# Layer with mLSTM and stick-breaking attention: gate rows computed from unit 35 on through small DRAM tensors, and k projected before q in the first half

## The chip, the core and the metric

The kernel runs on one core of one Trainium2 chip. The metric is device time in microseconds (us): the median of 3 runs, 694.9 us before the change (694.86 to 695.47). The names of the engines are those of the profile: PE is TensorE, DVE is VectorE, ACT is ScalarE, POOL is GpSimd; SP only issues DMAs. A trailing q (SPq, POOLq) marks the instruction queue of an engine.

## What is computed

One layer for 512 tokens of width 1024. The input is RMS-normed and projected by one wide matrix; two mixers work on the result, and their outputs are gated, summed, projected and added to the input.

```python
h = rmsnorm(x, norm_w)
(mq, mk, mv, mi, mf, mo, mz, sq, sk, sv, sz, gates) = split(h @ w_in + b_in)
# mLSTM: 4 heads of 256, q and k through a causal conv; 4 + 4 gate columns
log_i, log_f = mi, log_sigmoid(mf)
#   per head h~ = (decay-weighted q k^T) v / max(|den|, exp(-m_t)), m_t the running maximum
# stick-breaking attention: 8 heads of 128, q and k RMS-normed per head
qs, ks = rmsnorm(to_heads(sq), ..), rmsnorm(to_heads(sk), ..)
#   a[t,s] = sigmoid(z_ts) * prod_{s<j<t}(1 - sigmoid(z_tj)),  s < t
x = x + (g_m * (y_m @ w_proj_m) + g_s * (y_s @ w_proj_s)) @ w_out
```

What the change touches: the gate rows of the mLSTM (the running sum b of log_f, the running maximum m, and what is derived from them), and the order in which q and k of the first four attention heads are made.

## The kernel before

**Units.** All projections are cut into units of 24 matmuls of 128x128 by 128x512. Every fp32 operand is split into a high and a low fp32r part, and three products replace one (`mm3`, L90 to L93). A unit's weights, 512 KB, are loaded by SP into a tile `stg` (3 buffers, up to four units ahead); ACT copies the high part `wh` and DVE subtracts to get the low part `wl` (L96, L97), two units ahead of use. The units are, in this order: 0 to 3 q, 4 to 7 k, 8 to 11 v and 12 to 15 z of attention heads 0 to 3; 16 to 31 the same for heads 4 to 7; 32 to 51 o, z, v, q, k of the first mLSTM pair of heads; 52 to 71 the second pair; then the merge gates, the two branch projections and the output projection.

**What sets the order.** The program is written out in a hand-made order; each engine runs its own instructions in that order and waits only on semaphores. The loop at L1236 takes unit c: it evacuates the result of unit c-1, runs what was put off to this unit (`later`, `defer`), emits loads and splits ahead, then the first half of the unit's matmuls, then one step of every generator in `act` (attention heads, mLSTM heads, the gate chain; in the units of REST they pause), then the second half. So PE gets a few small matmuls of a generator between two halves of dense work. `pend` says from which unit a generator may start: `SB_START` for attention heads, `M_START` for mLSTM heads, and GATES_START = 4 for the gate chain `gates`.

**The gate chain before (L574 to L657).** Unit 4: 16 matmuls give the gate pre-activations as rows, 36 partitions by 512 tokens. Then, one step per unit: four PE transposes to 128 tokens by 16 (L592); Abs, Exp and Sigmoid on ACT; 21 small DVE instructions for the log-sigmoid (L603 to L612); four PE transposes back to rows (L616); two DVE scans over 512 tokens (L621, L626); differences, a split copy `rb2` of the row b - m; then eight PE transposes and one small matmul (L646 to L649) bring c = i - b, m and the block ends of b into columns (`c_lag`, `em`, `bs`). It ends in unit 10. Each mLSTM head then spreads its row of `rb2` over 128 partitions by one matmul with a selector `sel` (L751) and a DVE copy (L753); POOL masks it (L758), ACT exponentiates.

**q and k of the attention heads.** `qk_group` adds the bias (L346) into token-major tiles; ACT squares them, POOL makes the reciprocal norms `rq`, `rk`; k is scaled on DVE (L368), q's norm goes into the sigmoid's scale later. To use them a head needs them turned. Most are turned by `turn` (L381): DVE transposes 32x32 blocks into `ty`, 16 DMAs of 32 KB move the blocks to `tz`, and the head splits from there. In the set TURNED k of heads 0 and 1 is missing: those two heads turn k by four PE transposes each (L437).

Of the kernel before, what the change touches and what calls it, by code (L numbers as in the profile page):

```python
# [15 lines left out]
T = 512  # L16
# [10 lines left out]
SB_START = [10, 13, 16, 20, 26, 28, 32, 34]  # L27
M_START = [52, 56, 70, 76]
GATES_PREP, GATES_START = 3, 4
TURNED = {("q", 0, 0), ("q", 0, 1), ("q", 1, 0), ("q", 1, 1), ("k", 0, 1), ("k", 1, 1)}  # L30
# [5 lines left out]
def tile_hybrid_layer(  # L36
# [27 lines left out]
    tiny = pool("tiny", 4)  # L64
    psd = pool("psd", 4, space=bass.MemoryType.PSUM)
# [252 lines left out]
    class SbSet:  # L318
# [18 lines left out]
        def qk_group(self, name, c0):  # L337
# [4 lines left out]
            def evac(tb, ps):  # L342
# [6 lines left out]
                def norm():  # L349
# [8 lines left out]
                    if name == "q":  # L358
# [3 lines left out]
                        if tb == TB - 1:  # L362
                            defer(1, lambda: self.turn(name, 0))
                    else:
                        def scale():
# [3 lines left out]
                            if tb == TB - 1:  # L369
                                done.add(("k", self.s))  # L370
                                defer(1, lambda: self.turn(name, 1))
                        defer(1, scale)

                if tb < 2 or name == "q" and self.s == 0:
                    norm()
                else:
                    defer(1, norm)

            tok_group(w_in, c0 + 512 * self.s, h_sta, evac, name == "q" and self.s == 0, c0 + 512 * self.s, row)

        def turn(self, name, g):  # L381
# [8 lines left out]
            def move():  # L390
# [152 lines left out]
    sel = cst.tile([128, NH, 128], FR, name="sel")  # L543
    rb2 = cst.tile([128, T], FR, name="rb2")
# [6 lines left out]
    def gates_fill():  # L551
        wg = blk("P5", FR, (KT, 128), name="wg")
        nc.gpsimd.memset(wg.bitcast(F32), 0.0)

        sel32 = blk("y", shape=(NH, 128), name="sel32", p=36)
        nc.gpsimd.memset(sel32, 1.0)
        for r in (slice(0, 4), slice(32, 36)):
            nc.gpsimd.affine_select(out=sel32[r], in_=sel32[r], compare_op=OP.is_equal, fill=0.0, base=0,
                                    channel_multiplier=1, pattern=[[-1, 4], [0, 128]])
        nc.gpsimd.memset(sel.bitcast(F32), 0.0)  # L560
        nc.gpsimd.memset(rb2.bitcast(F32), 0.0)
        wg_t.extend([wg, sel32])

    def gates_prep():
        wg, sel32 = wg_t
# [5 lines left out]
        nc.vector.tensor_copy(sel[0:4], sel32[0:4])  # L571
        nc.vector.tensor_copy(sel[32:36], sel32[32:36])

    def gates():  # L574
# [12 lines left out]
        gi = g2[0:4, :]  # L587
        yield

        fp = att_ps()  # L590
# [7 lines left out]
        nc.vector.tensor_copy(f, fp[:, 0:16])  # L598
# [13 lines left out]
        nc.vector.scalar_tensor_tensor(f, f, 0.0, u, op0=OP.min, op1=OP.subtract)  # L612
        yield
        lp = att_ps()
        for j in range(TB):
            nc.tensor.transpose(lp[0:4, j * 128:(j + 1) * 128], f[:, 4 * j:4 * j + 4], ident)  # L616
        f = row("gl")
        nc.vector.tensor_copy(f, lp[0:4, :])
        yield
        m = row("gm")  # L620
        nc.vector.tensor_tensor_scan(m, f, gi, 0.0, op0=OP.add, op1=OP.max)  # L621
        msk = row("gk")
        nc.vector.memset(msk, 1.0)
        nc.vector.memset(msk.rearrange("p (b t) -> p b t", b=TB)[:, :, 0:1], 0.0)
        b = row("gp")
        nc.vector.tensor_tensor_scan(b, msk, f, 0.0, op0=OP.mult, op1=OP.add)  # L626
        yield
        rb = row("gu")
        nc.vector.tensor_tensor(rb, b, m, op=OP.subtract)
        nc.vector.tensor_copy(rb2[0:4], rb)  # L630
        nc.vector.tensor_tensor(rb2[32:36], rb, rb2[0:4].bitcast(F32), op=OP.subtract)
        c = row("gw")
        nc.vector.tensor_tensor(c, gi, b, op=OP.subtract)
# [669 lines left out]
```

## Time and profile before

| | us |
|---|---|
| median of 3 runs | 694.9 |
| profiled execution | 695.12 |
| its span, first to last instruction | 693.4 |
| PE busy | 684.5 |
| DVE busy | 472.9 |
| ACT busy | 334.6 |
| POOL busy | 122.3 |

The span is what the views of the profile cover; the profiled execution's time is 1.7 us longer than it. Matmuls are pipelined: a matmul's shown duration (some 390 ns for 512 columns) overlaps the next one's, so what an instruction takes of PE's time is read from the distance between the starts of neighbours, not from its duration.

### The profile page before, as it was taken

To read this page: it belongs to the slowest core of one execution; us is meant where nothing else is said; L and a number is where in the kernel's file an instruction comes from. 1 tells how busy PE (TensorE), PEld (TensorE's weight loads), DVE (VectorE), ACT (ScalarE), POOL (GpSimd) and SP (SyncE) were. 2 spreads that over 40 slices of the span, in tenths; PEclk is the share of its full clock that TensorE was granted. 3 is DMA by queue.
4 is the path that set the end of the run, shared out by engine and by line. 5 is a ranking of instruction groups with operands and counts; after the bars stand their busy time and mean duration, and the time that the engine had idled before them with its cause. 6 is when DMAs were issued, how large, how long until landed. Compare 5 with 4: busy or idle time off the path is not lost.

```text
span 693.4 us, 9382 instructions
## 1 busy us (share of the span) xinstructions
PE 684.5 (99%) x3172; PEld 569.9 (82%) x3172; DVE 472.9 (68%) x835; ACT 334.6 (48%) x629; POOL 122.3 (18%) x273
## 2 busy tenths in 40 slices
PE   7999999999999999999999999999999999999997
PEld 5888788888888888888888888888888888888876
DVE  6847997867997884479844738995353364445996
ACT  6244355475554643244466434447554343344451
POOL 5422122265440310000011110001112000111021
PEclk9999999999999999999999999999999999999999
DMA  7423534525553534333332343433223456579334
GB/s 248 138 88 104 149 117 124 150 61 159 153 150 99 144 107 133 92 91 92 91 92 61 82 116 99 115 92 104 79 61 87 118 174 199 159 169 217 124 83 130
DMA packets 111288, 84.10 MB, mean 121 GB/s; under 512 B 8302, under 2 KB 95240, under 8 KB 111240
## 3 DMA queue, kind: packets, MB, share of 16 engines
q1 hardware_dynamic: 108312, 76.82, 38.7%
q0 software_dynamic: 2784, 6.56, 4.9%
q8 instruction: 25, 0.41, 0.2%
q14 instruction: 23, 0.19, 0.1%
q10 hardware_dynamic: 144, 0.13, 0.1%
HBM read 65.12 MB, written 2.10 MB: 97 GB/s over the span
## 4 chain that ended last, share of the span: by engine, by line
PE 88%; DVE 1%; DMA 1%; ACT 0%; issue 0%; DVEq 0%; SPq 0%
PE dps L91 26%; PE dps L92 26%; PE dps L93 26%; PE aps L92 3%; PE aps L93 3%; PE aps L91 3%; DMA stg<-in_w_in_dram 1%; PE aps L805 1%; PE aps L807 1%; PE aps L806 1%; PE aps L437 0%; DVE wl L97 0%; DVE gp L626 0%; DVE gm L621 0%; PE aps L751 0%; DVE kraw L368 0%
## 5 line engine op out<-in xcount | busy, mean ns | idle before, releaser
L97 DVE TENSOR_TENSOR wl<-stg,wh 128x1024 fp32r<-128x1024 f32 x92 | 112.4, 1221 | 105.9 <-ACT wh L96 105.5
L91 PE MATMUL dps<-hh,wh 128*128 128x512 f32 x448 | 175.0, 391 | 0.0
L93 PE MATMUL dps<-hh,wl 128*128 128x512 f32 x448 | 174.5, 389 | 0.0
L92 PE MATMUL dps<-hl,wh 128*128 128x512 f32 x448 | 174.4, 389 | 0.0
L96 ACT ACTIVATE wh<-stg 128x1024 fp32r<-128x1024 f32 x92 | 96.8, 1052 | 58.8 <-PE dps L93 35.1
L93 PEld LDWEIGHTS dps<-hh,wl 128*128 128x128 f32 x448 | 84.1, 188 | 17.8
L91 PEld LDWEIGHTS dps<-hh,wh 128*128 128x128 f32 x448 | 84.1, 188 | 16.9
L92 PEld LDWEIGHTS dps<-hl,wh 128*128 128x128 f32 x448 | 84.2, 188 | 16.8
L91 PE MATMUL dps<-wh,hh 128*128 128x512 f32 x224 | 87.9, 393 | 0.0
L93 PE MATMUL dps<-wh,hl 128*128 128x512 f32 x224 | 87.3, 390 | 0.0
L92 PE MATMUL dps<-wl,hh 128*128 128x512 f32 x224 | 87.3, 390 | 0.0
L93 PEld LDWEIGHTS dps<-wh,hl 128*128 128x128 f32 x224 | 42.0, 188 | 9.0
L91 PEld LDWEIGHTS dps<-wh,hh 128*128 128x128 f32 x224 | 42.1, 188 | 8.3
L92 PEld LDWEIGHTS dps<-wl,hh 128*128 128x128 f32 x224 | 42.1, 188 | 8.2
L697 DVE SCALAR_TENSOR_TENSOR acc<-tmp,vec,acc 128x511 f32<-128x511 f32 (+2 forms) x48 | 36.0, 750 | 1.7
L700 ACT ACTIVATE tmp<-acc 128x512 f32<-128x512 f32 x16 | 10.1, 634 | 50.8 <-DVE acc L697 50.8
L462 POOL TENSOR_SCALAR_AFFINE_SELECT om<-om 128x128 f32<-128x128 f32 x32 | 16.4, 513 | 95.7 <-ACT om L460 95.6
L758 POOL TENSOR_SCALAR_AFFINE_SELECT w_all<-om 128x128 f32<-128x128 f32 x16 | 6.0, 410 | 153.9 <-DVE om L753 136.8
L468 DVE TENSOR_TENSOR_SCAN om<-om 128x512 f32<-128x512 f32 (+3 forms) x32 | 26.7, 833 | 4.6 <-POOL om L462 4.6
L460 ACT ACTIVATE om<-aps,rq 128x512 f32<-128x512 f32 (+3 forms) x32 | 16.8, 525 | 21.0 <-PE aps L93 20.9
L91 PE MATMUL dps<-yh,wh 128*128 128x512 f32 x64 | 24.9, 389 | 0.0
L92 PE MATMUL dps<-yl,wh 128*128 128x512 f32 x64 | 24.9, 389 | 0.0
(275 smaller groups left out, 1233.6 us busy)
## 6 DMA issues: line engine op xcount, KB each, us to landing
stg<-in_w_in_dram SPq DMA_DIRECT2D x87, 512.0 KB, 3.8
az<-ay SPq DMA_DIRECT2D x128, 40.0 KB, 2.5
stg<-in_w_proj_s_dram SPq DMA_DIRECT2D x8, 512.0 KB, 4.2
B<-in_w_out_dram SPq DMA_DIRECT2D x8, 512.0 KB, 4.5
stg<-in_w_proj_m_dram SPq DMA_DIRECT2D x8, 512.0 KB, 3.7
wl<-stg POOLq DMA_DIRECT2D x8, 512.0 KB, 5.6
tz<-ty SPq DMA_DIRECT2D x72, 32.0 KB, 1.9
brow<-in_b_in_dram SPq DMA_DIRECT2D x8, 256.0 KB, 5.4
```

What stands on the lines that cost most here:

```text
L91: nc.tensor.matmul(ps, ah, bh, start=first, stop=False)
L92: nc.tensor.matmul(ps, ah, bl, start=False, stop=False)
L93: nc.tensor.matmul(ps, al, bh, start=False, stop=last)
L96: nc.scalar.activation(hi, src, AF.Copy)
L97: nc.vector.tensor_tensor(lo, src, hi.bitcast(F32), op=OP.subtract)
L460: nc.scalar.activation(om[:, 0:n], zp, AF.Sigmoid, scale=rn[:, h:h + 1])
L462: nc.gpsimd.affine_select(out=om[:, ts], in_=om[:, ts], compare_op=OP.is_gt, fill=1.0, base=0, channel_multiplier=1, pattern=[[-1, 128]])
L468: nc.vector.tensor_tensor_scan(back, back, back, 1.0, op0=OP.mult, op1=OP.bypass)
L697: nc.vector.scalar_tensor_tensor(acc[:, j:], t[:, 0:T - j], cw(3 - j, ch), acc[:, j:], op0=OP.mult, op1=OP.add)
L700: nc.scalar.activation(t, acc, AF.Sigmoid)
L805: nc.tensor.matmul(nm[:, 0:258], ph, vh, start=j == 0, stop=False)
L806: nc.tensor.matmul(sum_v, ph, vl, start=False, stop=False)
```

## The change

**Gates.** The 16 gate matmuls stay in unit 4 but now stand at its head, not in its middle; the two groups of rows go to DRAM (`i_d`, `f_d`). The rest moves into a generator `gates_scan` that starts at unit 35. Every change of layout in it is a DMA through a small DRAM tensor with 4-byte elements (`by_token`, and the rows read back from `l_d`) in place of the PE transposes; the block ends come as broadcasts of `b_d`. Each mLSTM head reads its row of `rb_d` as one broadcast DMA to 128 partitions; `sel` and `rb2` go.

**q and k.** Units 0 to 3 now project k of the first four heads and units 4 to 7 q. k of heads 0 and 1 joins TURNED, so it is turned by DVE and DMA; half of the DMAs of all turns of the first half are issued by POOL. Head 0 starts at unit 11, not 10.

```diff
-SB_START = [10, 13, 16, 20, 26, 28, 32, 34]
+SB_START = [11, 13, 16, 20, 26, 28, 32, 34]
-GATES_PREP, GATES_START = 3, 4
+GATES_PREP, GATES_START, GATES_SCAN = 3, 4, 35
+TURNED = {..., ("k", 0, 0), ...}
+    dp = pool("dp", space=bass.MemoryType.DRAM)
...
-                        q = nc.gpsimd if self.s and a % 2 else nc.sync
+                        q = nc.gpsimd if a % 2 else nc.sync
...
+        nc.sync.dma_start(i_d, g2[0:4, :])
+        nc.sync.dma_start(f_d, g2[32:36, :])
+    def by_token(dst, src):
         for j in range(TB):
-            nc.tensor.transpose(fp[:, 4 * j:4 * j + 4], g2[32:36, j * 128:(j + 1) * 128], ident[32:36, 32:36])
+            nc.sync.dma_start(dst[:, 4 * j:4 * j + 4], src[:, j * 128:(j + 1) * 128].rearrange("h p -> p h"))
+    def gates_scan():
+        by_token(f, f_d)
...
+        nc.sync.dma_start(l_d, f)
         for j in range(TB):
-            nc.tensor.transpose(lp[0:4, j * 128:(j + 1) * 128], f[:, 4 * j:4 * j + 4], ident)
+            nc.sync.dma_start(f[:, j * 128:(j + 1) * 128], l_d[:, 4 * j:4 * j + 4].rearrange("p h -> h p"))
+        nc.sync.dma_start(gi, i_d)
...
+        for d, src in ((c_d, c), (m_d, m), (b_d, b), (rb_d, msk)):
+            nc.sync.dma_start(d, src)
+        by_token(c_lag[0].rearrange("p j h -> p (j h)"), c_d)
...
-            rp = att_ps()
-            nc.tensor.matmul(rp, sel[:, hd, :], rb2, start=True, stop=True)
-            nc.vector.tensor_copy(rbc[:, 0:T], rp)
+            nc.sync.dma_start(rbc[:, 0:T], bass.AP(tensor=rb_d.tensor, offset=rb_d.offset + T * hd,
+                                                   ap=[[0, 128], [1, T]]))
...
+    sets[0].qk_group("k", C_SK)
     sets[0].qk_group("q", C_SQ)
-    sets[0].qk_group("k", C_SK)
```

Three places show how the rows of the engines change. The first is PE in the middle of unit 10, before the change; `gw` and `gm` are the rows c and m of the gate chain, `kraw` is k of head 0:

```order
L647 MATMUL aps_865<-ident_84,gm_747 128x4
L649 MATMUL aps_874<-ones4_818 128x16
L437 MATMUL aps_887<-ident_84,kraw_685 128x128 x2
L437 MATMUL aps_887<-ident_84,kraw_706 128x128 x2
L91 MATMUL dps_754<-wh_727,hh_96 128x512
L92 MATMUL dps_754<-wl_728,hh_96 128x512
```

The same place after the change, where one half of the unit's dense work meets the other:

```order
L92 MATMUL dps_718<-wh_705,hh_98 128x512
L93 MATMUL dps_718<-wl_706,hh_98 128x512
L94 MATMUL dps_718<-wh_705,hl_99 128x512
L92 MATMUL dps_725<-wh_705,hh_98 128x512
L93 MATMUL dps_725<-wl_706,hh_98 128x512
```

Nothing stands between the halves any more: the eight gate transposes, the small matmul and the four transposes of k are gone. The second place is SP around unit 38, before; `stg` are weight loads, `az` moves the attention weights of a head:

```order
L504 DMA az_2925<-ay_2794 32x320 x8
L116 DMA stg_2954<-in_w_in_dram 128x2x512
L504 DMA az_2925<-ay_2794 32x320 x8
L116 DMA stg_3005<-in_w_in_dram 128x8x128
L116 DMA stg_3050<-in_w_in_dram 128x8x128
```

And after:

```order
L511 DMA az<-ay 32x320 x8
L616 DMA l_d<-gf 128x16
L117 DMA stg<-in_w_in_dram 128x2x512
L511 DMA az<-ay 32x320 x8
L117 DMA stg<-in_w_in_dram 128x8x128
L626 DMA gfi<-l_d 4x128x1 x4
L627 DMA gfi<-i_d 4x512
L117 DMA stg<-in_w_in_dram 128x8x128
```

The store of the log-sigmoid, which needs DVE's result, now stands ahead of a weight load and of half of the last attention head's moves; four element-wise DMAs stand ahead of the next load but one. The third place is DVE in units 38 and 39, before:

```order
L97 TENSOR_TENSOR wl<-stg,wh 128x1024
L539 TENSOR_TENSOR ys<-aps,ys 128x512
L683 SCALAR_TENSOR_TENSOR tmp<-dps,bvec,tmp 128x512
L684 SCALAR_TENSOR_TENSOR ym<-tmp,vec,ym 128x512
L97 TENSOR_TENSOR wl<-stg,wh 128x1024
```

And the start of the same piece after:

```order
L98 TENSOR_TENSOR wl<-stg,wh 128x1024
L546 TENSOR_TENSOR ys<-aps,ys 128x512
L606 TENSOR_SCALAR gw<-gu 128x16
L607 RECIPROCAL gw<-gw 128x16
L608 TENSOR_TENSOR gu<-gu,gw 128x16
L609 TENSOR_TENSOR gw<-gu 128x16
```

The 21 small instructions of the log-sigmoid, which stood in unit 7, now lie between `ys` and the next z evacuation.

## Rows read from the trace of the kernel before

**Rows 1.** The page: busy time of the engines.

```profile
PE 684.5 (99%) x3172; PEld 569.9 (82%) x3172; DVE 472.9 (68%) x835; ACT 334.6 (48%) x629; POOL 122.3 (18%) x273
```

**Rows 2.** Waits of PE (engine line <- releaser: total us, times, longest), the last of five.

```profile
PE aps L437 <- DVE kraw L368: 0.3, 1, 0.3
```

**Rows 3.** Timeline of PE: start us, us, engine line op out<-in xcount [idle before].

```profile
36.73 0.39 PE L91 MATMUL dps<-wh,hh 128*128 128x512 f32 x1
...
37.41 0.39 PE L91 MATMUL dps<-wh,hh 128*128 128x512 f32 x1
...
48.29 0.39 PE L93 MATMUL dps<-wh,hl 128*128 128x512 f32 x1
...
49.28 0.40 PE L92 MATMUL dps<-wl,hh 128*128 128x512 f32 x1
...
59.73 0.39 PE L93 MATMUL dps<-wh,hl 128*128 128x512 f32 x1
...
60.62 0.39 PE L92 MATMUL dps<-wl,hh 128*128 128x512 f32 x1
...
76.52 0.39 PE L93 MATMUL dps<-wh,hl 128*128 128x512 f32 x1
...
78.55 0.33 PE L437 MATMUL aps<-ident,kraw 128*128 128x128 f32 x1 [0.35 <-DVE kraw L368]
...
78.96 0.39 PE L92 MATMUL dps<-wl,hh 128*128 128x512 f32 x1
...
96.84 0.34 PE L93 MATMUL aps<-ktt,qtt 128*128 128x384 f32 x1
...
97.68 0.39 PE L92 MATMUL dps<-hl,wh 128*128 128x512 f32 x1
...
345.06 0.40 PE L93 MATMUL dps<-hh,wl 128*128 128x512 f32 x1
...
345.75 0.39 PE L92 MATMUL dps<-hl,wh 128*128 128x512 f32 x1
```

**Rows 4.** Timeline of DVE, same columns: unit 3, unit 7, units 38 to 43.

```profile
36.35 0.19 DVE L569 TENSOR_TENSOR wg<-gst,wg 128x32 fp32r<-128x32 f32 x1
...
54.23 0.17 DVE L603 TENSOR_SCALAR gw<-gu 128x16 f32<-128x16 f32 x1
...
58.49 0.17 DVE L612 SCALAR_TENSOR_TENSOR gf<-gf,gu 128x16 f32<-128x16 f32 x1
...
258.66 1.22 DVE L97 TENSOR_TENSOR wl<-stg,wh 128x1024 fp32r<-128x1024 f32 x1
...
263.38 0.75 DVE L683 SCALAR_TENSOR_TENSOR tmp<-dps,bvec,tmp 128x512 f32<-128x512 f32 x1 [2.85 <-ACT tmp L682]
...
288.77 1.23 DVE L97 TENSOR_TENSOR wl<-stg,wh 128x1024 fp32r<-128x1024 f32 x1 [3.53 <-ACT wh L96]
```

**Rows 5.** Timeline of ACT: the table load of the gate chain, unit 38.

```profile
49.74 1.28 ACT L601 ACT_TABLE_LOAD   x1
...
256.48 0.69 ACT L682 ACTIVATE tmp<-dps,bvec 128x512 f32<-128x512 f32 x1 [2.98 <-PE dps L93]
```

**Rows 6.** Timeline of PE: the first dense matmul of unit 40.

```profile
267.90 0.39 PE L91 MATMUL dps<-wh,hh 128*128 128x512 f32 x1
```

**Rows 7.** Line L621: duration of a scan, ns min/median/max.

```profile
L621 DVE TENSOR_TENSOR_SCAN gm<-gl,g x1: 1204/1204/1204, 68.0 to 68.0; 4x512 f32<-4x512 f32 x1
```

**Rows 8.** DMA issues: line, count, KB each, median us to landing.

```profile
stg<-in_w_in_dram SPq DMA_DIRECT2D x87, 512.0 KB, 3.8
...
tz<-ty SPq DMA_DIRECT2D x72, 32.0 KB, 1.9
brow<-in_b_in_dram SPq DMA_DIRECT2D x8, 256.0 KB, 5.4
```

**Rows 9.** Tile tz on POOL: issue duration ns, and landing of its DMAs.

```profile
L397 POOL DMA_DIRECT2D tz<-ty x24: 533/547/804, 156.2 to 193.0; - x24
...
DMA to landing us min/median/max: 1.7/2.9/4.7
```

More of the change, by code (lines that the diff above doesn't have):

```diff
@@ L370, in scale @@
                                 done.add(("k", self.s))
-                                defer(1, lambda: self.turn(name, 1))
+                                if self.s == 0:
+                                    defer(1, lambda: self.turn(name, 0))
+                                defer(2 - self.s, lambda: self.turn(name, 1))
                         defer(1, scale)
-                if tb < 2 or name == "q" and self.s == 0:
+                if name == "q" and tb == TB - 1:
+                    if self.s:
+                        defer(2, lambda: self.turn(name, 0))
+                    else:
+                        self.turn(name, 0)
+                if tb < 2 or name == "k" and self.s == 0:
                     norm()
@@ L377, in evac @@
                     defer(1, norm)
-            tok_group(w_in, c0 + 512 * self.s, h_sta, evac, name == "q" and self.s == 0, c0 + 512 * self.s, row)
+            tok_group(w_in, c0 + 512 * self.s, h_sta, evac, name == "k" and self.s == 0, c0 + 512 * self.s, row)
         def turn(self, name, g):
@@ L542, in tile_hybrid_layer @@
     NH = 4
-    sel = cst.tile([128, NH, 128], FR, name="sel")
-    rb2 = cst.tile([128, T], FR, name="rb2")
+    i_d, f_d, c_d, m_d, b_d, rb_d = [dp.tile([NH, T], F32, name=n)
+                                     for n in ("i_d", "f_d", "c_d", "m_d", "b_d", "rb_d")]
+    l_d = dp.tile([128, 16], F32, name="l_d")
     c_lag = [cst.tile([128, TB, NH], F32, name=f"c_lag{k}") for k in range(TB)]
@@ L553, in gates_fill @@
         nc.gpsimd.memset(wg.bitcast(F32), 0.0)
[L555 to L562, printed above, removed]
+        wg_t.append(wg)
     def gates_prep():
-        wg, sel32 = wg_t
+        wg = wg_t[0]
         for c in range(2):
@@ L612, in gates, with rows @@
         nc.vector.scalar_tensor_tensor(f, f, 0.0, u, op0=OP.min, op1=OP.subtract)
+        nc.sync.dma_start(l_d, f)
         yield
-        lp = att_ps()
-        for j in range(TB):
-            nc.tensor.transpose(lp[0:4, j * 128:(j + 1) * 128], f[:, 4 * j:4 * j + 4], ident)
-        f = row("gl")
-        nc.vector.tensor_copy(f, lp[0:4, :])
+        yield
+        def rows(name):
+            t = sp.tile([NH, 2, T], F32, name=name, tag="A", bufs=4)
+            return t[:, 0, :], t[:, 1, :]
@@ L619, in gates @@
+        f, gi = rows("gfi")
+        for j in range(TB):
+            nc.sync.dma_start(f[:, j * 128:(j + 1) * 128], l_d[:, 4 * j:4 * j + 4].rearrange("p h -> h p"))
+        nc.sync.dma_start(gi, i_d)
+        m, msk = rows("gmk")
+        nc.gpsimd.memset(msk, 1.0)
+        nc.gpsimd.memset(msk.rearrange("p (b t) -> p b t", b=TB)[:, :, 0:1], 0.0)
         yield
-        m = row("gm")
+        yield
+        b, c = rows("gbc")
         nc.vector.tensor_tensor_scan(m, f, gi, 0.0, op0=OP.add, op1=OP.max)
-        msk = row("gk")
@@ L630, in gates @@
[L630 to L633, printed above, removed]
-        ones4 = row("ones4")
-        bend = ones4[:, 128:144].rearrange("p (x h) -> p x h", h=NH)
-        ones4 = ones4[:, 0:128]
-        for h in range(NH):
-            nc.vector.tensor_scalar(bend[:, :, h:h + 1],
-                                    b.rearrange("p (x t) -> p x t", x=TB)[:, :, 127:128],
-                                    ident[0:4, h:h + 1], None, op0=OP.mult)
@@ L1202, in tile_hybrid_layer @@
     act = []
-    pend = [(GATES_START, 1, lambda: True, gates)]
+    pend = [(GATES_SCAN, 1, lambda: True, gates_scan)]
+    later.setdefault(GATES_START, []).append(gates)
     for s in (0, 1):
```

36 lines of the change are left out of this document (11 added, 25 removed).

## The prediction

> **What bounds the kernel now.** I read the page's busy times first. PE is busy 684.5 us of a span of 693.4 us [rows 1], and no other engine comes near. Then the list of PE's waits: it has five lines; four belong to the warm-up and the turning of x at the very start, before the second unit, and the last is one wait of 0.3 us in which head 0's transposes stand still for k's scaling [rows 2]. So behind the start PE never stops, and what counts is the time from one matmul's start to the next. In the timeline, four starts in unit 4 lie at 36.73 to 37.41 us: 0.227 us a step of 512 columns [rows 3]. A matmul taken from PE's row moves everything after it forward, as long as weights, evacuations and DMAs keep up; one added anywhere else costs nothing while its engine has idle time there.
>
> **What the change takes from PE.** At each place I take the distance between the last dense matmul before the small ones and the second dense one after them (the first one after a transpose starts late, so it has to be inside), less the two steps that stay, 0.45 us [rows 3]:
> - Unit 5, four transposes of the forget gate: 49.28 - 48.29 = 0.99, less 0.45: 0.54 us.
> - Unit 7, four transposes back: 60.62 - 59.73 = 0.89, less 0.45: 0.44 us.
> - Unit 10, eight gate transposes, the small fp32 matmul and head 0's four k transposes with the 0.35 us wait for k's scaling among them: 78.96 - 76.52 = 2.44, less 0.45: 1.99 us.
> - Unit 13, head 1's four k transposes: 97.68 - 96.84 = 0.84, less a 384-column step (three quarters of 0.227, 0.17) and a full one: 0.44 us.
> - Four selector matmuls, one in each mLSTM head: 345.75 - 345.06 = 0.69, less 0.45: 0.24 us; times four 0.96 us.
>
> The sum is 4.4 us (0.54 + 0.44 + 1.99 + 0.44 + 0.96). Nothing is added to PE: the 16 gate matmuls move inside unit 4 and stay. Against the profiled execution that is 695.12 - 4.4 = 690.7 us with a span near 689.0; the median of the three runs lies 0.2 us lower, so 690.5 us.
>
> A transpose's shown duration would give more: the one at 78.55 us lasts 0.33 us, while in unit 5 four of them cost 0.54 us in all [rows 3]. The Trainium skill (TensorE: Matmul & The Clock Gate, Part 4: PE-mode transpose) gives about 275 ns for a 128x128 transpose inside a kernel. By that, 24 transposes would be 6.6 us and the sum some 8 us. The trace's starts disagree, at 0.11 to 0.13 us each; they are what I use.
>
> **What it puts elsewhere, and what hides it.** *Unit 4.* The gate matmuls now need the split gate weights `wg` at the unit's head. DVE ends them at 36.35 + 0.19 = 36.54 us and PE is there at 36.73 [rows 3, 4]. DVE's rows ahead of them gain the scaling of k's first block, four small instructions that stand in front of a split whose ACT half comes later anyway; I take zero, with 0.5 us as the other end.
>
> *Head 0 at unit 11.* Its second step was at unit 12 before too, since 11 is a resting unit, so its scores keep their place. Its q is now made in units 4 to 7, moved in unit 9, weighted in unit 11 and needed by PE in the middle of unit 12. Half of the 16 moves goes through POOL: 8 x 0.547 = 4.4 us of issuing, and the slowest such landing of the second half's took 4.7 us [rows 9]. Moves that start when unit 9's norms are done, some 5 us into it, end 5 + 4.4 + 4.7 = 14 us behind its start; PE's need lies three and a half units of at least 24 x 0.227 = 5.4 us behind it, 19 us. The cover is 5 us less the weighting and the splits, 2 to 3 us of DVE and ACT. I take zero. POOL's reciprocal norm of q's last block stands behind these issues, and the sigmoids that read it come still later.
>
> *Units 35 to 46, ACT and DVE.* ACT gets three small activations and two table loads of 1.28 us [rows 5], 3.2 us with the 0.2 us instructions; it is idle for 2.98 us just before unit 38's evacuation [rows 5], so 0.2 us is left over. The 21 DVE instructions took 58.49 + 0.17 - 54.23 = 4.4 us; they now lie ahead of a z evacuation in front of which DVE idles 2.85 us [rows 4], so that evacuation and the split behind it come 1.6 us later. Two scans of 1.20 us [rows 7] and two 512-wide differences of 0.75 us (as L683) make 3.9 us in front of a split with 3.53 us of idle time [rows 4]: 0.4 us late. Who waits for that is PE, by the weights: the split for unit 40 ends at 258.66 + 1.22 = 259.88 us and unit 40 starts at 267.90 [rows 4, 6], 8.0 us of slack. 1.6 and 0.4 us disappear in it.
>
> *The same units, SP and the DMA queues.* SP waits at the store `l_d` for the 21 instructions; behind it stand a weight load and eight moves of the last attention head. They leave some 4.4 us late. `gfi` and the stores of c, m, b and b - m hold SP once more, each for a landing of about 1.9 us [rows 8] or for the scans. Then the element-wise DMAs: 20 of them, 512 elements of 4 bytes each. No row shows 4-byte moves. The nearest: a weight load, most of them 1024 runs of 512 bytes, lands in 3.8 us and a move of 64 such runs in 1.9 us [rows 8]; 960 more runs, 60 more on each of 16 engines, cost 1.9 us, so 32 ns a run on an engine. As an estimate from these two rows a DMA of 512 runs spread over all 16 engines takes 1.0 us of them, four in a row 4 us: with the wait at `l_d` 8.4 us, about the 8.0 us of slack if the load itself had none of its own; but a load is issued a unit and more before its split. Below this price lies nothing that could gain. I take zero stall here, and 2 us as the upper end of what an even spread can do.
>
> *mLSTM heads.* The row of b - m is a 256 KB broadcast from DRAM; the nearest row is `brow`, the same shape, 5.4 us to landing [rows 8]. Its readers are POOL's masks and, one unit (5.4 us) later, ACT's exponentials; PE reads the product two units on. DVE loses four copies. I take zero, both ways.
>
> **Rivals.**
> 1. *A partial stall.* One of the covers above is too small: head 0's q is late by a slow POOL issue, or ACT, DVE and SP together push a split past its 8.0 us. For it: the 2.98, 2.85 and 3.53 us of idle time are all just filled. Against it: the delays found do not add up on one instruction. It costs 1 to 3 us: 691.5 to 693.5 us.
> 2. *Slower: the row-wise elements on few engines.* `gfi` reads four rows back into four partitions. If each of the four DMAs runs on four engines only, one per row, an engine takes 4 x 128 runs x 32 ns = 16.4 us, and the next weight loads queue behind that on those engines. With the wait of 4.4 us at `l_d` ahead this is 20.8 us against 8.0 us of slack, so PE could stand up to 12.8 us in units 41 to 46: at the worst 703 us. It turns into a loss from 8.0 + 4.4 = 12.4 us of delay on. Against it: between issue and split a load has over a unit of time besides, and the wait at `l_d` and the elements hit different loads. A middle value is 696.5 us.
> 3. *The transposes were worth more.* If a transpose is worth its 0.275 us, 24 of them and the five other matmuls give 8 us: 687 us. Against it stand the starts in [rows 3].
> 4. *Nothing gained.* PE's row is shorter, but another engine sets the pace behind it, and the time stays within 0.2% of 694.9. Against it: after the start PE waits once in the whole trace [rows 2], and DVE is at 68% [rows 1].
>
> The Trainium skill (DMA: Bandwidth & Descriptors, Rules for kernel authors) speaks against this part of the change: a strided last dimension becomes one descriptor per element, and a DMA whose outermost dimension is under 16 is confined to as many engines. By that, rival 2's four engines is the case for `gfi`, and the other 16 DMAs, with 128 partitions outermost, use all 16; what an element costs then decides, and no row here shows it.
>
> **How the numbers follow.** About 0.2%, 1.4 us, is what a measurement of this kernel can tell from no change. The forecast, 690.5 us, give or take half a microsecond for the reading of the starts, gets 0.76; the partial stall 0.12 (most of it still faster by over 0.2%, 0.03 of it not); the slower case 0.05; the cheaper PE 0.02; nothing gained 0.05. So faster 0.87, same 0.08, slower 0.05. For eight in ten the range runs from 689.5 us, just under the forecast, to 692.6 us, which takes in the unit 4 wait of 0.5 us and most of the partial stall.
>
> **What would show it.** PE's list of waits has no line at units 4, 11 or 12 and none after unit 35; PE's busy time falls by about 4 us and the span to 689; units 5, 7, 10 and 13 are shorter by the amounts above. Right in mechanism but wrong in size would be a wait of PE for `wg` in unit 4 or for `qtt` in unit 12. Wrong would be waits for `wl` or for an evacuation between 270 and 310 us, with long landings of the loads behind `gfi`; then rival 2 or 1 has it. If PE's starts at the five places close up and the span does not follow, another engine took over, and its wait is in the list.

## Result and the profile after

The changed kernel takes 696.66 us (median of 22 runs, 694.79 to 698.07) against 695.16 us before (22 runs): a ratio of 1.0020, 95% interval 1.0014 to 1.0026. It is 1.5 us slower, where 690.5 us was forecast, and its runs lie 3.3 us apart, those of the kernel before 1.7 us. The first profiled execution after took 695.63 us, with a span of 693.9 us against 693.4 us.

The page of the profile after, engine busy times (answers to [rows 1]), and PE's list of waits (answers to [rows 2]; engine line <- releaser: total us, times, longest):

```profile
PE 682.0 (98%) x3142; PEld 567.0 (82%) x3142; DVE 467.4 (67%) x819; ACT 337.0 (49%) x631; POOL 133.1 (19%) x302
```

```profile
PE aps L93 <- DVE ktt L98: 1.9, 1, 1.9
PE dps L1163 <- DVE idle L1158: 1.5, 1, 1.5
PE aps L300 <- DVE x L290: 1.2, 1, 1.2
PE dps L1185 <- DVE hh L302: 0.8, 1, 0.8
PE dps L1187 <- DVE fl L1144: 0.7, 1, 0.7
PE aps L579 <- DVE wg L569: 0.3, 1, 0.3
PE dps L1187 <- POOL fl L1144: 0.3, 1, 0.3
```

Line numbers are those of the changed kernel, one to some ten higher than before. Two waits behind the start are new: 0.3 us for the gate weights `wg` in unit 4, and 1.9 us for `ktt`, the low part of head 1's k, in unit 14. Head 0's wait for `kraw` [rows 2] is gone. The rest belongs to the start. The wait in unit 14 in PE's timeline (start us, us, engine line op out<-in [idle before <-releaser]); the third row is unit 15's first dense matmul:

```profile
101.03 0.39 PE L92 MATMUL aps<-ktt,qtt 128*128 128x512 f32 x1
103.36 0.50 PE L93 MATMUL aps<-ktt,qtt 128*128 128x512 f32 x1 [1.94 <-DVE ktt L98]
...
107.39 0.39 PE L92 MATMUL dps<-hh,wh 128*128 128x512 f32 x1
```

And DVE's timeline ahead of it, from the weighting of q to the split that PE waits for:

```profile
81.52 0.75 DVE L408 TENSOR_SCALAR tz<-tz,qkw 128x1024 f32<-128x1024 f32 x1 [4.68 <-DMA tz<-ty]
...
84.53 1.28 DVE L422 TENSOR_TENSOR tmp<-dps,brow 128x512 f32<-128x512 f32 x2
...
92.81 1.22 DVE L475 TENSOR_TENSOR_SCAN om<-om 128x512 f32<-128x512 f32 x1 [1.15 <-POOL om L469]
...
96.48 0.77 DVE L408 TENSOR_SCALAR tz<-tz,qkw 128x1024 f32<-128x1024 f32 x1
...
102.62 0.69 DVE L98 TENSOR_TENSOR ktt<-tz,ktt 128x512 fp32r<-128x512 f32 x1
```

DVE first stands 4.68 us, until the moves of q's first half have landed. From 81.5 us on it works without a break but two (1.15 us, and 0.26 us for a `wh`) until `ktt` is done at 103.3 us. PE wanted it one step behind 101.03, at 101.26: it is 2.0 us late. In the kernel before the same split was 1.4 us early, done at 101.78 us for a matmul at 103.15 (DVE's and PE's timelines):

```profile
101.10 0.68 DVE L97 TENSOR_TENSOR ktt<-aps,ktt 128x512 fp32r<-128x512 f32 x1
```

```profile
103.15 0.39 PE L92 MATMUL aps<-ktt,qtt 128*128 128x512 f32 x1
```

ACT's timeline shows where the 1.15 us come from:

```profile
89.37 1.04 ACT L97 ACTIVATE wh<-stg 128x1024 fp32r<-128x1024 f32 x1
90.43 1.28 ACT L467 ACT_TABLE_LOAD   x1
91.72 0.69 ACT L467 ACTIVATE om<-aps,rq 128x512 f32<-128x512 f32 x1
```

The activation table of the sigmoids was loaded by the gate chain at 49.74 us before [rows 5]. That chain is now behind unit 35, so head 0's first sigmoid pays the load. At the same place in before DVE idled 0.18 us.

The late gate chain itself costs PE nothing. PE's distance to its place in before is +0.35 us at unit 35 and +0.36 us at unit 52. Its element-wise DMAs land in about the time of a move (issues: KB each, median us to landing):

```profile
gf<-f_d SPq DMA_DIRECT2D x4, 2.0 KB, 3.7
...
c_lag<-c_d SPq DMA_DIRECT2D x4, 2.0 KB, 3.4
bs<-b_d SPq DMA_DIRECT2D x4, 2.0 KB, 3.0
```

The table gives how far PE stands behind (+) or ahead of (-) the kernel before, in us, by the start of a unit's first dense matmul in PE's timeline; the last two columns are the end of PE's last matmul and the span. The other kernels are told of below.

| kernel | unit 5 | 11 | 14 | 15 | 52 | 87 | PE's end | span |
|---|---|---|---|---|---|---|---|---|
| changed, first profile | +1.32 | -1.74 | -1.89 | +0.35 | +0.36 | -0.74 | -0.6 | +0.5 |
| changed, profile e_again1 | +0.29 | -2.77 | -2.48 | +1.35 | +1.42 | +0.32 | +1.7 | +2.9 |
| gates alone (e_gates) | +0.58 | -1.99 | -1.95 | -1.96 | -1.96 | -3.06 | -3.0 | -2.5 |
| q and k alone (e_qk) | -0.12 | -1.08 | -1.51 | -0.70 | -0.68 | -0.69 | -0.2 | -0.2 |
| table early (e_table) | -0.10 | -3.16 | -2.94 | -1.98 | -1.99 | -3.09 | -1.3 | -0.1 |
| best (e_fuse8) | +0.01 | -3.05 | -3.43 | -2.65 | -2.64 | -3.74 | -3.7 | -2.6 |

The column of unit 5 holds chance too: e_stall, told of below, changes nothing before unit 13 and stands at +1.48 there. The span lies 1.1 us further behind than PE's end in the first profile. There the last store, 128 KB issued by ACT, takes 3.1 us to land against 2.0 us before, and its last nine packets of 144 come late. The transfers from 691.5 to 693 us, where the kernel before has none at the same place (queue, kind: packets, MB, share of 16 engines; q10 carries ACT's stores):

```profile
q10 hardware_dynamic: 9, 0.01, 2.0%
q14 instruction: 1, 0.01, 1.4%
```

One packet of 8 KB that loads instructions runs from 1.93 to 2.26 us behind the store's issue, and the nine start right behind it. All nine profiles whose last store takes 3.1 us or more show this packet and nine late ones. Before, e_qk, e_stall and e_sp have no such packet there, and the store lands in 2.0 us; e_h14, e_fixA and e_fixB have one, but there all packets of the store had started by then. That the packet holds the nine up is read off this order; it was not tried by a run.

### The profile page after: what moved, and what is told of

Read it like the earlier page. It is cut to its first block, busy times and chain, and to the rows that moved or that the text cites. A ratio compares the mean times of both kernels' runs of the same rounds, so it can differ in the third digit from the quotient of the medians.

```text
span 693.9 us, 9389 instructions
## 1 busy us (share of the span) xinstructions
PE 682.0 (98%) x3142; PEld 567.0 (82%) x3142; DVE 467.4 (67%) x819; ACT 337.0 (49%) x631; POOL 133.1 (19%) x302
## 4 chain that ended last, share of the span: by engine, by line
PE 89%; DVE 3%; POOL 2%; issue 2%; DMA 2%; ACT 1%; SPq 0%; DVEq 0%; POOLq 0%; ACTq 0%
PE dps L92 26%; PE dps L94 26%; PE dps L93 26%; PE aps L93 3%; PE aps L94 3%; PE aps L92 3%; POOL tz L404 1%; DMA P<-in_w_in_dram 1%; DMA brow<-in_b_in_dram 1%; PE aps L800 1%; PE aps L802 1%; PE aps L801 1%; DVE hl L306 1%; DVE wl L98 1%; POOL fl L1144 0%
## 5 line engine op out<-in xcount | busy, mean ns | idle before, releaser
L696 ACT ACTIVATE tmp<-acc 128x512 f32<-128x512 f32 x16 | 10.1, 633 | 50.8 <-DVE acc L693 50.8
L404 POOL DMA_DIRECT2D tz<-ty x56 | 30.8, 557 | 9.9 <-DVE ty L394 8.9
L469 POOL TENSOR_SCALAR_AFFINE_SELECT om<-om 128x128 f32<-128x128 f32 x32 | 14.3, 446 | 84.3 <-ACT om L467 84.2
L126 POOL DMA_DIRECT2D wl<-stg x8 | 7.1, 884 | 93.6 <-DVE yml L98 61.7
```

The lines of the kernel that those rows point to most:

```text
L126: nc.gpsimd.dma_start(out=self.wl, in_=self.st, accum_op=OP.add)
L404: q.dma_start(tz[32 * b:32 * b + 32, :, a, :], src[32 * a:32 * a + 32, b])
L469: nc.gpsimd.affine_select(out=om[:, ts], in_=om[:, ts], compare_op=OP.is_gt, fill=1.0, base=0, channel_multiplier=1, pattern=[[-1, 128]])
L696: nc.scalar.activation(t, acc, AF.Sigmoid)
```

## Experiments

Theory 1: PE's work shrank as forecast, but the gain is handed back where head 1's first scores wait for DVE. Rivals: the late chain costs time; the start costs it; a later place does (the expectations of e_a8 and e_fuse8 call this theory 3). Medians are compared with the kernel before as timed beside each (695.4 to 695.6 us).

### Each half alone

e_gates keeps q ahead of k, head 0 at unit 10, the transposes of k on PE and the moves of the first half with SP alone; `...` stands for lines left out, here and below:

```diff
-SB_START = [11, 13, 16, 20, 26, 28, 32, 34]
+SB_START = [10, 13, 16, 20, 26, 28, 32, 34]
...
-TURNED = {..., ("k", 0, 0), ...}
...
-    sets[0].qk_group("k", C_SK)
     sets[0].qk_group("q", C_SQ)
+    sets[0].qk_group("k", C_SK)
```

> Only the gate half of the change: the four gate rows go through DRAM from unit 35 on and the gate matmuls of both halves stand at the head of unit 4, while q stays ahead of k, head 0 starts at unit 10 and its k is still turned by PE. Theory 1 (the gain of the changed kernel is handed back where head 1's first scores wait for the VectorE split of its k): PE gains 0.54 + 0.44 + 0.27 us (units 5, 7 and the gate transposes in unit 10) = 1.3 to 2.3 us up to unit 13, loses 0.3 us or more to wg in unit 4, and then waits 1 to 2.5 us at head 1's first scores, because ScalarE loads its activation table late (1.28 us) and VectorE can't run ahead; about 695.5 us. Rival (nothing waits): 691.7 us. Rival 2 (the late gate chain costs time): the distance to the kernel before grows between units 35 and 48.

Measured: 692.92 us, 2.7 us faster than before (ratio 0.9963, 0.9951 to 0.9976), and no wait of PE behind the start; it lies between theory 1 (695.5) and the rival without a wait (691.7). The forecast of theory 1 fell here: the table load falls on head 0's first sigmoid here too, and DVE idles for it 1.15 us too, yet the split is ready (DVE's timeline):

```profile
81.95 1.28 DVE L416 TENSOR_TENSOR tmp<-dps,brow 128x512 f32<-128x512 f32 x2
...
90.24 1.23 DVE L469 TENSOR_TENSOR_SCAN om<-om 128x512 f32<-128x512 f32 x1 [1.15 <-POOL om L463]
...
99.22 0.68 DVE L98 TENSOR_TENSOR ktt<-aps,ktt 128x512 fp32r<-128x512 f32 x1
```

`ktt` is done 3.4 us earlier than in the changed kernel, 1.3 us ahead of PE's need: both weightings of q (63.5 and 70.6 us) and head 0's splits lie ahead of this stretch, and v's first bias adds (`tmp`) start at 81.95 instead of 84.53 us. The rival that the late chain costs time falls: the lead is -1.96 us at units 15 and 52.

e_qk is the other half: the kernel before with the lines of q and k of the diff, the gate chain at unit 4.

> Only the q and k half of the change: k ahead of q in the first half, head 0's k turned by VectorE and DMA, half of the moves issued by POOL, head 0 from unit 11 on; the gate chain is the one before, at unit 4. Theory 1: the table is loaded by the early gate chain, so VectorE loses only 0.8 us to the later split of q and up to 1 us to the wait for a move issued by POOL; PE gains 1.3 us (8 transposes fewer) and waits 0.5 to 1 us at head 1's first scores: about 694.5 us. Rival (no wait): 693.6 us. Rival (the q and k half alone brings the whole wait of 1.9 us): 695.8 us.

Measured: 695.11 us (0.9994, 0.9985 to 1.0003), 0.6 us above theory 1, with the wait that it named: PE waits 0.5 us for `ktt`, and unit 14 lasts 7.65 instead of 6.83 us. So one half gives 2.7 us, the other 0.5 us, which is not clear of no change, and both together lose 1.5 us. The split of head 1's k shows how they add up. It is 1.4 us early in before, 1.3 us early with the gates alone, 0.6 us late with q and k alone, and 2.0 us late with both. With the gates alone v's adds start 2.7 us earlier than in before (81.95 against 84.63 us), which takes up the table load; with q and k alone they start at 84.76 us and in the changed kernel at 84.53, behind the late weighting, and nothing takes it up.

### What delays DVE, taken away piece by piece

e_table loads the table in unit 6:

```diff
+    def table():
+        d = tiny.tile([128, 1], F32, name="dmy", bufs=1)
+        nc.scalar.activation(d, mhalf[:, 0:1], AF.Sigmoid)
+    later.setdefault(6, []).append(table)
```

> The changed kernel with one small Sigmoid on a 128 x 1 tile put on ScalarE in unit 6, so that the activation table of the sigmoids is loaded there and not at head 0's first gate (90.43 us). Theory 1: the 1.15 us that VectorE idles ahead of head 0's first scan go, PE's wait of 1.9 us at head 1's first scores shrinks to about 0.8 us, and the time falls by about 1.1 us, to 695.5 us. Rival (the table load is covered, VectorE is late through the wait for the moves alone): no change, 696.7 us.

Measured: 695.02 us (0.9997, 0.9987 to 1.0006), against before 2.1 us better than the changed kernel by the medians and 1.6 us by the ratios. The wait for `ktt` fell by 1.2 us, the load's length, and two others stand beside it (PE's waits):

```profile
PE dps L94 <- DMA wl<-stg: 1.4, 1, 1.4
...
PE aps L93 <- DVE ktt L98: 0.7, 1, 0.7
...
PE dps L92 <- DVE tmp L422: 0.4, 1, 0.4
```

The last is v's add, for which unit 12 waits, behind DVE's wait for q's moves. The first is at 644 us and has a part of its own below. The Trainium skill (ScalarE: Activation LUTs, What ACT_TABLE_LOAD costs) adds a drain of about 1.4 us to the 1.28 us of the load; the row of this load shows none: the next activation starts where the load ends (91.72 us), and DVE idled 1.15 us.

e_late puts the weighting of q's second half, which only head 2 needs, two units later:

```diff
-                defer(3, weight)
+                defer(3 if g == 0 or self.s else 5, weight)
```

> The changed kernel with the weight of q's second half (0.75 us on VectorE, needed by head 2 only) moved two units later, out of VectorE's queue ahead of head 1's splits. Theory 1 (VectorE's queue from 81.5 us to 103.3 us sets when head 1's first scores start): PE's wait falls from 1.9 to about 1.2 us, 695.5 to 696.0 us. Rival (the transfers set it): no change, 696.7 us.

Measured: 696.18 us (1.0009, 1.0000 to 1.0018), 0.2 us above its range. The wait for `ktt` is 1.2 us, as expected. 0.8 us stand at v's add, but that wait varies by itself: it is 0.4 and 0.6 us in two further profiles of the changed kernel and 0.9 us in e_a8, which leaves that place alone. Against before the median is 0.8 us better than the changed kernel's, the length of the weighting.

e_sp issues all moves of the first half from SP, none from POOL:

```diff
-                        q = nc.gpsimd if a % 2 else nc.sync
+                        q = nc.gpsimd if self.s and a % 2 else nc.sync
```

> The changed kernel with all moves of the first half's q and k issued by SP, as in the kernel before, and none by POOL. Theory 1: VectorE's first weight of q, which waited for the moves until 81.5 us, starts earlier by at most 1 us or later by as much as SP's longer list of issues costs (8 more of 0.6 us each per half); the wait at head 1's first scores changes by -1 to +1 us: 695 to 697.5 us. Rival (POOL's moves are the whole cause): no wait at head 1's first scores, 692.5 to 693 us.

Measured: 701.99 us (1.0097, 1.0080 to 1.0113), outside both expectations. SP's list is that much longer, the weighting of q waits until 85.01 us and the splits and v's adds behind it until 91.3 us (PE's waits, then DVE's timeline):

```profile
PE dps L92 <- DVE tmp L422: 7.8, 1, 7.8
```

```profile
85.01 0.75 DVE L408 TENSOR_SCALAR tz<-tz,qkw 128x1024 f32<-128x1024 f32 x1 [6.87 <-DMA tz<-ty]
88.94 1.23 DVE L98 TENSOR_TENSOR wl<-stg,wh 128x1024 fp32r<-128x1024 f32 x1 [3.17 <-ACT wh L97]
...
91.28 1.28 DVE L422 TENSOR_TENSOR tmp<-dps,brow 128x512 f32<-128x512 f32 x2
```

PE doesn't wait for q here. It waits for v's add, which waits in DVE's queue behind q's. That is the same mechanism as in the changed kernel, larger, and the granted clock (explained below) halves there as well, for some 7 us.

e_mid puts the gate matmuls back between the halves of unit 4:

```diff
-    later.setdefault(GATES_START, []).append(gates)
+        if c == GATES_START:
+            gates()
```

> The changed kernel with the gate matmuls between the two halves of unit 4, as in the kernel before, instead of at its head. Theory 1: the wait for the gate weights (0.33 us in the profiled run) goes, but the gain is handed back at head 1's first scores, where PE then waits longer by as much: 0 to 0.3 us in all, 696.4 to 696.7 us. Rival (the start sets the loss: PE's late arrival and the wait in unit 4 are carried to the end): 0.3 to 1.0 us faster, 695.7 to 696.3 us.

Measured: 696.49 us (1.0017, 1.0006 to 1.0028). The wait for `wg` is gone. The time lies where theory 1 had it, but against before it is 0.6 us better than the changed kernel by the medians and 0.2 us by the ratios, so that this run does not part theory 1 from the rival of the start. Its profile showed something else, which the next part takes up: unit 14 lasts 10.66 us, with the same 1.9 us wait as the 9.08 us of the first profile.

### What a wait costs

e_stall is the kernel before, with 18 small DVE instructions ahead of head 1's splits:

```diff
+    def busy():
+        d = tiny.tile([128, 4], F32, name="dmy", bufs=1)
+        nc.vector.memset(d, 1.0)
+        for _ in range(18):
+            nc.vector.tensor_tensor(d, d, d, op=OP.mult)
+    later.setdefault(13, []).append(busy)
```

> The kernel before with 18 small VectorE instructions on a 128 x 4 tile (2.7 to 3.4 us by the 0.15 to 0.19 us that such instructions take in the trace before) put into VectorE's queue in unit 13, ahead of head 1's splits, which had 1.1 us of slack there; all other work stays as it was. It makes the wait of the changed kernel by itself: PE should wait 1.6 to 2.3 us at head 1's first scores. Theory 1 with the clock (a wait of 2 us there lets TensorE's granted clock fall to half in some executions, as after the wait of the kernel with the gate matmuls between the halves of unit 4, where it was 0.50 from 104 to 107 us): the median rises by more than the wait, by 2.5 us or more, to 698 us, and the executions spread over 3 us. Rival (a wait costs its own length): 697.2 to 697.8 us with a spread of 1.3 us, as before.

Measured: 699.36 us, 3.9 us more (1.0059, 1.0044 to 1.0074), for a wait of 2.0 us. The four runs lie 1.3 us apart, not the 3 us expected: all of them show the fall described now, by a mean granted clock of 0.997 or less. The expectation counts DVE's slack to the first matmul of the scores, 1.1 us; the split is needed by the second, so it is 1.4 us. The granted clock is the share of TensorE's full 2.4 GHz that it may use. In the table of stretches (us, then busy time and count of PE, PEld, DVE, ACT, POOL, then PEclk, DMA share, GB/s) the granted clock is the third number from the end:

```profile
104.00:106.00 2.00, 0.79 (x4) 0.33 (x2) 1.90 (x3) 0.00 (x0) 0.00 (x0) 1.00 0.46 177
106.00:108.00 2.00, 1.23 (x5) 1.04 (x5) 2.00 (x4) 0.10 (x1) 0.00 (x0) 0.74 0.04 8
108.00:110.00 2.00, 2.00 (x8) 1.81 (x8) 2.00 (x7) 1.79 (x4) 1.01 (x4) 0.50 0.18 23
```

No matmul starts for 2.4 us, 2.0 us of it idle, and when PE starts again its clock falls from 2.4 to 1.2 GHz for some 3 us. Unit 14 lasts 10.70 us. It lasts 9.08 us in the first profile of the changed kernel, with the same wait and no such fall, and 6.83 us without a wait.

Two more profiled executions of the changed kernel, unchanged, ask whether this makes the 1.0 us between its first profile and its median (no diff):

> The changed kernel, unchanged, profiled again. Theory (clock): the granted clock falls to 0.5 for about 3 us behind the wait at head 1's first scores, unit 14 lasts 10.5 to 10.7 us instead of 9.08 us, and the time is 696.5 to 697.5 us. Rival (it lies elsewhere): unit 14 lasts 9.1 us again, and the stretch that differs from the first profile is the start (before unit 5) or units 102 to 104.

> As the run before it: unit 14 at 9.1 us or at 10.5 us and above, start and units 102 to 104 read beside it. By the theory at least one of the two shows the fallen clock behind the wait.

Measured: 698.28 and 699.92 us, one run each and above the 696.5 to 697.5 us expected; unit 14 lasts 10.67 and 10.65 us. The stretches of e_again1, and its waits behind the start:

```profile
100.00:102.00 2.00, 0.83 (x4) 0.36 (x2) 1.90 (x3) 0.00 (x0) 0.00 (x0) 1.00 0.39 152
102.00:104.00 2.00, 1.24 (x6) 1.14 (x7) 2.00 (x4) 0.46 (x1) 0.00 (x0) 0.85 0.02 4
104.00:106.00 2.00, 2.00 (x8) 1.71 (x8) 2.00 (x7) 1.43 (x4) 1.44 (x5) 0.50 0.20 26
106.00:108.00 2.00, 2.00 (x9) 1.58 (x8) 1.79 (x4) 0.00 (x0) 0.75 (x2) 0.80 0.78 278
108.00:110.00 2.00, 2.00 (x11) 1.63 (x10) 0.84 (x2) 1.41 (x2) 0.00 (x0) 1.00 0.24 66
```

```profile
PE aps L93 <- DVE ktt L98: 1.9, 1, 1.9
PE dps L94 <- DMA wl<-stg: 1.0, 1, 1.0
PE dps L92 <- DVE tmp L422: 0.4, 1, 0.4
```

So the same wait of 1.9 us costs 2.25 us in the first profile and 3.8 us here. Of six profiles with such a wait in unit 14, four show the fallen clock. The 22 timed runs tell how often: 3.4 us at half the clock take 0.0025 off its mean over the span. Ten runs show a mean of 0.997 or less, as 7 of the 91 runs of before timed beside the experiments do, four show 0.998, and eight 0.999 or more, which leaves no room for the fall. The first profile is one of the eight. The medians are 697.1 us for the ten and 696.2 us for the eight, so that the clock is a part of the loss and not all of it. In six of the 22 runs the time is also 2.0 to 3.2 us longer than the span, where each of the 91 has 1.7 or 1.8; what makes that stays open. Both the expected place and one of the rival's places are real, since the wait for `wl` near 644 us is there too.

### The last accumulated piece

The low parts of the last eight projection pieces are made by a DMA that POOL issues and that adds into `wl`. The last one lands 5.6 us after its issue in before and 5.5 us in e_gates, but 8.9 us in the first profile after, 10.1 us in e_again1 and 10.6 us in e_table. The transfers of 5 us behind its issue, in e_again1 (638 to 643 us, from 0.9 us behind it) and then in before (637 to 642 us, from 0.2 us behind it; queue, kind: packets, MB, share of 16 engines; q0 carries POOL's, q1 SP's):

```profile
q1 hardware_dynamic: 680, 1.27, 84.6%
q0 software_dynamic: 23, 0.09, 9.4%
```

```profile
q0 software_dynamic: 254, 0.91, 92.3%
q1 hardware_dynamic: 89, 0.16, 10.9%
```

SP loads into a buffer once an accumulation has freed it. In e_again1 the last but one lands at 636.5 us, SP issues seven loads (`B` and six `xr`) from 636.6 to 639.6 us, and the last accumulation, issued at 637.15 us, shares the engines with them. In before the last but one lands only at 640.0 us, and the same loads follow 3.2 us behind the last one's issue (636.83 us). From the third of the eight on every second one is long in each trace, and which ones are long differs between the two; what settles that was not tried. e_a8 has the last piece split by DVE:

```diff
-    for un in units[n_proj - 8:]:
+    for un in units[n_proj - 8:n_proj - 1]:
```

> The changed kernel with the last of the eight projection pieces whose low part a POOL DMA accumulates split by VectorE instead, as the other 92 are. Theory 3 (a second place near 644 us: the accumulating DMA lands 9 us after its issue and PE waits for it in a part of the executions, and loses clock by the wait): 0.5 to 1 us faster than the changed kernel, 695.6 to 696.2 us. Rival (in the profile of the changed kernel that place costs 0.1 us, so all of its loss comes from unit 14): no change, 696.7 us.

Measured: 696.46 us (1.0013, 1.0003 to 1.0022), 0.4 us better against before than the changed kernel, between theory 3 and the rival and too little to tell them apart. The place costs 0.1 us in the first profile of the changed kernel, 1.0 and 1.3 us in its two others and 1.4 us in e_table; how much of the median loss it makes, this run does not tell.

### Moving the heads, and the mended kernel

e_h14 starts head 1 at unit 14, with no other edit. e_fixA has the table early, q's weightings later, and heads 0 and 1 at 12 and 14; e_fixB the same with 12 and 13:

```diff
-SB_START = [11, 13, 16, 20, 26, 28, 32, 34]
+SB_START = [12, 14, 16, 20, 26, 28, 32, 34]
...
-                defer(3, weight)
+                defer(3 if self.s else 4 if g == 0 else 5, weight)
```

> The changed kernel with head 1 starting one unit later (14 instead of 13). Theory 1 (what is handed back is only the wait at head 1's first scores): no wait there, PE is 1.9 us ahead of before from unit 15 on and stays so, the granted clock stays at 1.00 there, and the time is 692.5 to 693 us. Rival (the loss is in the shared supply of VectorE and moves on): a wait of 1 us or more appears at the first scores in unit 15, 695.5 us or more.

> The changed kernel with the table loaded in unit 6, the weight of q's first half put one unit later (behind v's bias adds on VectorE), that of its second half two units later, and heads 0 and 1 started one unit later each (12 and 14). Theory 1 (VectorE's queue between 80 and 103 us, fed late by the moves, is what hands the gain back): no wait in units 11 to 15, PE 3.4 us ahead of before at unit 16; with head 1 close to head 2 as in the kernel with head 1 alone moved, which lost 2.2 us again between units 15 and 28, 691 to 693 us. Rival (the loss moves on whatever the start units): 694 us or more.

> The same with head 1 left at unit 13, so that heads 0 and 1 start in neighbouring units. Theory 1: head 1's splits now stand ahead of head 0's second pair of row blocks on VectorE, so that its first scores don't wait, and head 2 is no closer than before: all of the 4.4 us that PE no longer has to do are kept, 690.5 to 692 us. Rival (VectorE and ScalarE can't feed two heads in neighbouring units): 0.5 to 2 us of waits in units 13 to 16, 692.5 to 694.5 us.

Measured: e_h14 693.70 us (0.9976, 0.9967 to 0.9986), e_fixA 696.29 us (1.0013, 1.0004 to 1.0023), e_fixB 696.26 us (1.0010, 1.0001 to 1.0020). Unit 14's wait went in all three. e_h14 is the best of them, 0.7 us above its range: in its profile it leads by 1.8 us from unit 21 to 25 and by 1.2 us from unit 28 on, and waits 1.2 us for `wl` near 644 us. e_fixA led by 4.4 us at unit 15, of which 1.4 us was work of the two heads only put off (3.0 us at unit 20). At unit 28 it is 0.5 us behind (PE's waits, e_fixA):

```profile
PE dps L92 <- DVE kraw L347: 1.9, 1, 1.9
...
PE aps L444 <- DVE kraw L367: 0.9, 2, 0.5
```

These lie in units 24 and 26: DVE idles 4.16 us at 160 us for a bias broadcast (`brow`) from SP's queue. By the order of SP's queue I take it that the moved heads' own transfers stand in front of it; that was not tried apart. The rival (the loss moves on) was right for e_fixA; e_fixB missed both of its ranges.

e_fuse leaves the heads where the changed kernel has them, loads the table early, and has no separate weighting pass: ACT's copy takes the weight as its scale and DVE's subtraction multiplies, in four pieces.

```diff
...
-            if name == "q":
-                defer(3, weight)
...
-                if name == "q" and not (name, self.s, h // 2) in TURNED:
+                if name == "q":
                     nc.scalar.activation(th, tp, AF.Copy, scale=qkw)
-                    nc.vector.scalar_tensor_tensor(tl, tp, qkw, th.bitcast(F32), op0=OP.mult, op1=OP.subtract)
+                    turned = (name, self.s, h // 2) in TURNED
+                    for x in range(TB) if turned else (slice(None),):
+                        nc.vector.scalar_tensor_tensor(tl[:, x], tp[:, x], qkw, th.bitcast(F32)[:, x],
+                                                       op0=OP.mult, op1=OP.subtract)
...
```

> The changed kernel with the table loaded in unit 6 and without the two or four separate VectorE passes that multiply the turned q by its weight: the weight goes into the two steps of the split (ScalarE's copy with a scale, and VectorE's subtraction as four pieces of 128 x 128), so that VectorE neither does 0.75 us per half nor waits for the moves ahead of its other work; heads 0 and 1 start as in the changed kernel. Theory 1 (the queue of VectorE between 80 and 103 us is what hands the gain back): about 1 us less of VectorE's work ahead of head 1's first scores on top of the 1.15 us of the table, no wait above 0.3 us in units 11 to 14, and no new one behind, since the heads stay where they are; 691 to 692.5 us, spread 1 us. Rival (the moves' arrival near 80 us sets it): PE still waits 0.5 us or more in unit 11 and 0.5 us or more in unit 14: 694 us or more.

> The kernel with the weight folded into the split and the table early, and with the last of the eight pieces split by VectorE too. Theory 3: the wait of 0.2 us and more at 642 us goes, PE keeps the 3.5 us of unit 87 to the end, 692.0 to 693.0 us with a spread below 1 us. Rival (VectorE, busy 9 tenths there, only puts its own wait in that place): 693.8 us or more.

Measured: e_fuse 693.81 us (0.9979, 0.9969 to 0.9988), above its range, with 0.4 us at `ktt` and a wait for `wl` near 642 us. e_fuse8, with the last piece split by DVE as well, 692.81 us (692.52 to 693.25; 0.9962, 0.9947 to 0.9976), as theory 3 said. It and e_gates beat the kernel before by as much (2.6 and 2.7 us); e_fuse8 leads by more at PE's end and has one wait left, 0.5 us at `ktt`. Its profile adds up: 4.6 us of PE's work are gone, unit 14 takes 0.8 us more than before and the last store 1.1 us, which leaves 2.7 us; the span is 2.6 us shorter.

## Why the prediction was wrong

- **What PE loses: right.** Units 5, 7, 10 and 13 are shorter by 0.56, 0.47, 2.03 and 0.43 us and each mLSTM head by 0.27 us, 4.6 us in all against the 4.4 us of the sum. PE's busy time fell by 2.5 us only, where about 4 was named: up to unit 5 it is 1.0 us more than before (42.16 against 41.14 us), and 0.35 us of the sum was idle time.
- **Unit 4: its other end.** PE waited 0.3 us for `wg` in the first profile, where zero was taken and 0.5 us named. In e_mid it is gone, for a gain too small to tell (0.2 to 0.6 us). The start of unit 5 lies -0.1 to +1.8 us from before's over all kernels with late gates, which is more than the wait; since e_stall, with the gates where they were, stands at +1.5, most of it can come without late gates. What makes it stays open.
- **Head 0 at unit 11: the step that failed.** The sum asked whether q is there when PE needs it, found 2 to 3 us of cover, and took zero. PE indeed never waited for `qtt`, and the moves were no later than worked out: the weighting started 12.6 us behind unit 9's start (68.88 us), where 14 us had been taken. But the weighting that waits for the moves stands in DVE's queue, and behind it stand head 0's splits, v's adds, the scans and head 1's splits. DVE idled 4.68 us and was done with them at 103.3 us, 2.0 us past PE's need. The prediction named who waits for q, not what is queued behind the waiting instruction, and so put at zero what measured 2.25 us in the first profile and 3.8 us in e_again1.
- **Units 35 to 46, ACT: a term left out.** Two table loads were counted where the chain goes, none where it leaves. The load it no longer does at 49.74 us falls on head 0's first sigmoid, on the path to head 1's split: DVE idles 1.15 us, and without it the wait is 1.2 us shorter (e_table). With DVE at 68% over the span, the stretch from 81 to 103 us, where it is full, was not looked at. e_gates shows that the load alone stalls nothing; with q's later splits and weightings it does.
- **Units 35 to 46, SP and DMA: right,** and rival 2 fell. PE has no wait there, and the 4-byte DMAs land in 3.0 to 3.7 us.
- **Rivals.** The first (a cover too small, q late by POOL's moves) came near at 0.12, with 1 to 3 us. It looked for the wait at head 0's q in unit 12; it came at head 1's k in unit 14, through DVE's queue, and took 2.25 us in the first profile and 3.8 us in e_again1. The fourth (another engine sets the pace) describes it as well: from 81 to 103 us DVE does.
- **What no rival had.** A wait of 2 us costs another 1.6 us where the clock falls, by the mean clocks in some 10 to 14 of the 22 runs. The last store takes 1.1 us longer, so the span ends 5.05 us behind PE's last matmul instead of 3.9: in the first profile PE's end is 0.6 us ahead of before's, and the span is 0.5 us longer all the same. Eight other profiles show 5.0 to 5.2 us, six 3.9 or 4.0, e_gates 4.4. Which kernels get the packet of instructions there stays open.
- **The balance of e_again1.** Against before its start costs 0.3 us, the wait for v's add and unit 12 0.7, unit 14 3.8, units 15 to 51 0.1, the wait for `wl` and what follows it 1.3, the last store 1.25; the work that is gone gives 4.6. The sum is 2.9 us, the span's distance.

## What to carry to other kernels

Ask of a step that waits not only who needs its result, but what stands behind it in its engine's queue, in the stretch where that engine is full, not by its share of the span. When a piece of work moves away, look for what it did in passing for others: here it had loaded an activation table. And a gain on the engine that sets the pace counts only if the next stages can follow: two halves that gave 2.7 and 0.5 us alone lost 1.5 us together, since the 1.4 us by which a split had been early were used up by the one, and the table load of the other, harmless alone, then made PE wait. And look past the place that was changed: the last store alone took back 1.1 us.

## What the runs showed of the hardware

- TensorE's granted clock fell from 2.4 to 1.2 GHz for about 3 us when PE started again after 1.9 to 2.0 us of idle time (no start for 2.3 to 2.4 us), in four of six profiles, which costs 1.6 us. In the other two (unit 14 of 9.08 and 9.06 us) it stayed.
- With loads of SP in flight and more issued from 0.6 us ahead on, a DMA of POOL got 9.4% of the engines' time in a stretch of 5 us behind its issue, against 92.3% where they came 3.2 us later; its landing went from 5.6 to 10.1 us.
- DMAs of 512 elements of 4 bytes, four in a row, land in 3.0 to 3.7 us (medians of three groups), as a 32 KB move does in this kernel (2.9 and 3.1 us).
- Nine of the 144 packets of a store started only behind an 8 KB packet that loads instructions, and the store landed in 3.1 us instead of 2.0; nine of 17 profiles show it.
